# The modulation's products in four column quarters, and the state space part's transposes in one row

## The chip, the cores and the metric

The kernel runs on one core of one Trainium2 chip. The metric is the device time of one execution in microseconds. Three executions took 2125.67 to 2131.05 us, median 2130.01. A further execution was recorded by the hardware profiler; all durations below come from it.

TensorE does the matrix products and writes PSUM. VectorE (DVE), ScalarE (ACT) and GpSimd (POOL) work beside it, SyncE (SP) and GpSimd issue DMAs.

## The reference

Two layers of a diffusion trunk over 128 context tokens and 1024 latent tokens, 1024 features wide. What the change touches:

```python
def ada_mod(cvec, w, b):
    m = jax.nn.silu(cvec) @ w + b
    shift, scale, gate = jnp.split(m, 3, axis=-1)
...
    sh_p, sc_p, g_p = ada_mod(c_ctx[None], w_ada[l], b_ada[l])
    sh_s, sc_s, g_s = ada_mod(c, w_ada[l], b_ada[l])
    hp = rms_norm(xp, norm_w[l]) * (1.0 + sc_p) + sh_p
    hs = rms_norm(xs, norm_w[l]) * (1.0 + sc_s) + sh_s
```

So for each of the two layers two conditioning vectors of 1024 go through a matrix of 1024 x 3072. The first layer holds a bidirectional state space mixer with 16 heads of 64 in 128-token chunks:

```python
    y_diag = jnp.einsum('bhcls,bcshp->bclhp', scores, xdt)
    ...
    y_off = jnp.einsum('bclhn,bchpn->bclhp', cc, new_states[:, :-1]) * jnp.exp(acs).transpose(0, 2, 3, 1)[..., None]
    return (y_diag + y_off).reshape(b, L, h, p), new_states[:, -1]
```

and beside it a long convolution, an input projection and an output projection. The second layer is neighbourhood attention. All is fp32.

## The kernel before, in words

Activations are kept with features on the partitions, 1158 token columns in three pieces of 386. A projection multiplies weight tiles of 128 x 128 with these pieces. Each fp32 operand is split into a high and a low part of the type fp32r; three products (L158 to L160: high-high, high-low, low-high) replace one fp32 product.

The projections run as foreground. Everything else of the first layer is written as generators in a list `bg`; after each piece of a projection `tick` adds a rate to a credit and advances the first generator by as many steps as the credit holds. The finished order on each engine is then set by a scheduler that follows the dependences.

**The modulation.** Its matrix is cut into 24 blocks (12 for each layer) of 256 output columns, each in two halves of 512 input features, 128 partitions by 4 x 256. `ada_mm` keeps a column pair of the conditioning as the stationary operand and moves 256 weight columns. For the first eight blocks of layer 0 (`ada_block`, L295) the products are plain fp32, 8 per block, at the program's start: they give the shift and scale for the norm of the first layer's input. For the other 16 blocks `ada_gen` runs in the background of the projection of z. It splits each weight half into fp32r parts (L259 on ScalarE, L260 on VectorE) and does two products for each of 8 slices (L303, L304), with the conditioning's high and low part side by side as four stationary columns. `ada_row` (L309) copies the result, 2 or 4 rows of 256, to SBUF; for the gate of layer 1 it is also stored in DRAM (growd) for the last stage, `final`. `ada_cols` (L320) multiplies the rows with a small selection matrix, which sums high and low parts and turns rows into columns, and adds the bias.

At the start ScalarE squares the eight input tiles and VectorE adds them up (xacc, L1500); L340 sums them over the features, L355 spreads the reciprocal root over the partitions (`rstd_rep`), `make_h` makes the projection's operands, and L185 to L187 are the first projection.

**The state space part.** `ssd` runs in the background of the projection of x0 and the gate. For each chunk and each half of the heads it computes the part from the carried states with tokens on the partitions: two products (L1005), scaled and added on VectorE (yo, L1006 and L1008). This must be turned to features on the partitions. L1033 does so by a plain fp32 product with the identity, one for each pair of heads, into the PSUM bank yT, and the two products of that pair inside the chunk (L1037) accumulate on top, each into 64 partitions. Each group of four heads has its own masked decay on VectorE before that (ga, from the products L1014). L1038 reads the whole bank. Chunk 0, the context, has no carried state and no L1033.

Of the kernel before, what the change touches and what calls it, by code (L numbers as in the profile page):

```python
# [44 lines left out]
class Net:  # L45
# [148 lines left out]
    def open(self):  # L194
# [18 lines left out]
        self.sel4 = self.t(self.p_c, [4, 2], "sel4")  # L213
# [12 lines left out]
        self.growd = self.t(d, [4, 1024], "growd")  # L226
# [4 lines left out]
    def silu_c(self):  # L231
# [6 lines left out]
        s = self.cs = self.t(self.p_c, [128, 8, 2], "csl")  # L238
        nc.vector.scalar_tensor_tensor(out=s, in0=th, scalar=1.0, in1=c, op0=ALU.add, op1=ALU.mult)
        nc.vector.tensor_scalar(out=s, in0=s, scalar1=0.5, scalar2=None, op0=ALU.mult)  # L240
        self.ca = self.t(self.p_c, [128, 8, 4], "ca", F32R)
        nc.vector.tensor_copy(self.ca[:, :, 0:2], s)
        nc.vector.tensor_tensor(out=self.ca[:, :, 2:4], in0=s, in1=self.ca[:, :, 0:2].bitcast(F32), op=ALU.subtract)

    def ada_gen(self, blocks, pool):

        nc = self.nc
        todo = [(l, nb, half) for l, nb in blocks for half in range(2)]

        def load(i):  # L250
            r = self.t(pool, [128, 1024], "u8", bufs=self.nu8)
            l, nb, half = todo[i]
            self.dma(r, self.i["wada"][l, nb, half])
            return r
# [8 lines left out]
        raw = {0: load(0), 1: load(1)}  # L263
        yield
        hl = {0: split(0, raw.pop(0))}
        raw[2] = load(2)
        yield
        hl[1] = split(1, raw.pop(1))
        yield
        last = None  # L270
        for i, (l, nb, half) in enumerate(todo):
            if i + 3 < len(todo):
                raw[i + 3] = load(i + 3)
            if i + 2 < len(todo):
                hl[i + 2] = split(i + 2, raw.pop(i + 2))
            yield
            hi, lo = hl.pop(i)
            if half == 0:
                p = self.ps()
            self.ada_mm(p, half, hi, lo)  # L280
            if last:
                self.ada_cols(*last)
                last = None
            if half:
                last = l, nb, self.ada_row(l, nb, p, pool)
        self.ada_cols(*last)

    def ada_block(self, nb, raw, pool):

        nc = self.nc  # L290
        p = self.ps()
        for half, r in enumerate(raw):
            for k in range(4):
                kk = half * 4 + k
                nc.tensor.matmul(p[0:2, :256], self.cs[:, kk, :], r[:, k * 256:(k + 1) * 256], start=(kk == 0), stop=(kk == 7))  # L295
        return 0, nb, self.ada_row(0, nb, p, pool, 2)

    def ada_mm(self, p, half, hi, lo):
        nc = self.nc
        for k in range(4):  # L300
            kk = half * 4 + k
# [4 lines left out]
    def ada_row(self, l, nb, p, pool, n=4):  # L306

        row = self.t(pool, [4, 256], "w3")[0:n]
        self.nc.scalar.copy(row, p[0:n, :256])  # L309
# [4 lines left out]
    def ada_cols(self, l, nb, row):  # L314

        nc = self.nc
        n = row.shape[0]
        q = self.ps()
        for j in range(2):
            nc.tensor.matmul(q[:, 2 * j:2 * j + 2], row[:, j * 128:(j + 1) * 128], self.sel4[0:n], start=True, stop=True)  # L320
# [636 lines left out]
    def ssd(self, pool):  # L957
# [4 lines left out]
        for c in list(range(1, NCH)) + [0]:  # L962
# [35 lines left out]
            for g in range(2):  # L998
                yT = self.ps()
                if c:  # L1000
# [8 lines left out]
                    yield  # L1009
# [733 lines left out]
def constants():  # L1743
    import numpy as np

    f = np.float32
# [111 lines left out]
```

## Time and profile before

| | us |
|---|---|
| median of three executions | 2130.01 |
| profiled execution | 2134.96 |
| its span, first to last instruction | 2133.2 |
| TensorE busy | 2084.8 (98%) |
| VectorE busy | 1355.3 (64%) |
| ScalarE busy | 942.2 (44%) |
| GpSimd busy | 121.4 (6%) |

The program's start, with the first eight blocks, is about the first 90 us of the span. The 16 background blocks run from 334 to 441 us, the state space part from 883 to 1209 us, the attention from about 1455 us on. A plain fp32 matmul of the program leaves two records in the trace; an fp32r matmul leaves one. Matmuls are pipelined, so the time that one takes from TensorE's stream is the distance from its start to the next start, not its duration.

### The profile page before, as it was taken

What the parts mean: (1) busy time and instruction counts of PE and PEld (TensorE: products, weight loads), DVE (VectorE), ACT (ScalarE), POOL (GpSimd) and SP (SyncE); (2) the same over time, 40 slices, a digit from 0 to 9 for tenths busy, and PEclk for the clock granted to TensorE, in tenths of its full rate; (3) what the DMA queues carried; (4) which work ended last, traced back from release to release, by engine and by line L of the source; (5) the groups of instructions that cost most, each with busy time, mean ns of one, the idle gap of its engine ahead of it and who ended that gap; (6) DMA issues with size and microseconds to landing.
All of it is one profiled execution on the core that took longest, in us unless ns stands there. A gap on an engine that the chain in (4) does not pass through costs nothing.

```text
span 2133.2 us, 34117 instructions
## 1 busy us (share of the span) xinstructions
PE 2084.8 (98%) x13152; PEld 1870.8 (88%) x13152; DVE 1355.3 (64%) x2804; ACT 942.2 (44%) x2063; POOL 121.4 (6%) x241
## 2 busy tenths in 40 slices
PE   7999999999999999999999999999999999999998
PEld 3899998889999999888887899998888888888977
DVE  5797756544787778888788784563444444454364
ACT  3576553544233232554456621434444544543231
POOL 1110000010000000000000100200000000000000
PEclk8999999999999999999999999999999999999999
DMA  8133335765122113343334351243333223333452
GB/s 325 51 120 105 116 135 204 232 189 206 66 74 73 66 67 100 130 134 121 103 130 138 113 186 50 68 124 95 91 103 83 77 88 94 112 115 104 126 211 79
DMA packets 114945, 256.22 MB, mean 120 GB/s; under 512 B 27047, under 2 KB 63419, under 8 KB 112319
## 3 DMA queue, kind: packets, MB, share of 16 engines
q1 hardware_dynamic: 99472, 191.38, 28.8%
q0 software_dynamic: 15312, 62.67, 8.2%
q8 instruction: 104, 1.70, 0.3%
q14 instruction: 57, 0.47, 0.1%
HBM read 186.61 MB, written 67.38 MB: 119 GB/s over the span
## 4 chain that ended last, share of the span: by engine, by line
PE 36%; issue 21%; DMA 2%; DVE 2%; ACT 1%; POOL 1%; SPq 0%; POOLq 0%; DVEq 0%; ACTq 0%
PE pj L158 7%; PE pj L159 7%; PE pj L160 7%; PE bg L1037 1%; PE bg L1005 1%; PE pj L1377 1%; PE pj L1376 1%; PE pj L1378 1%; PE bg L1033 1%; PE bg L1014 1%; DMA yr<-yad 1%; PE bg L930 1%; PE bg L1339 1%; PE bg L1351 1%; DMA ycd<-X 1%
## 5 line engine op out<-in xcount | busy, mean ns | idle before, releaser
L158 PE MATMUL pj<-hh,whi 128*128 128x386 f32 x1728 | 603.0, 349 | 0.5 <-DVE acc L862 0.5
L159 PE MATMUL pj<-hl,whi 128*128 128x386 f32 x1728 | 590.2, 342 | 0.0
L160 PE MATMUL pj<-hh,wlo 128*128 128x386 f32 x1728 | 587.6, 340 | 0.0
L158 PEld LDWEIGHTS pj<-hh,whi 128*128 128x128 f32 x1728 | 326.4, 189 | 15.7 <-issue 12.9
L159 PEld LDWEIGHTS pj<-hl,whi 128*128 128x128 f32 x1728 | 326.7, 189 | 7.3 <-issue 6.2
L160 PEld LDWEIGHTS pj<-hh,wlo 128*128 128x128 f32 x1728 | 326.4, 189 | 3.5 <-issue 2.7
L131 DVE TENSOR_TENSOR wlo<-wraw,whi 128x1024 fp32r<-128x1024 f32 x108 | 131.8, 1222 | 165.5 <-ACT whi L130 158.9
L130 ACT CAST whi<-wraw 128x1024 fp32r<-128x1024 f32 x108 | 113.1, 1048 | 246.3 <-PE pj L159 213.3
L1255 DVE CUSTOM_DVE_ANT_0 sz<-bg,Tb 128x512 f32<-128x512 f32 x128 | 83.5, 688 | 127.8 <-PE bg L1322 127.2
L598 ACT COPY raw<-pj 128x386 f32<-128x386 f32 x105 | 50.5, 483 | 169.7 <-PE pj L160 82.6
L1257 ACT ACTIVATE sz<-sz,mx 128x512 f32<-128x512 f32 x128 | 91.5, 716 | 56.2 <-DVE mx L1255 56.0
L158 PE MATMUL pj<-yhi,whi 128*128 128x386 f32 x324 | 110.3, 340 | 1.4 <-DVE x L1094 1.4
L159 PE MATMUL pj<-ylo,whi 128*128 128x386 f32 x324 | 110.9, 342 | 0.0
L160 PE MATMUL pj<-yhi,wlo 128*128 128x386 f32 x324 | 110.4, 341 | 0.0
L1353 ACT COPY Pt<-bg 128x512 f32<-128x512 f32 (+1 forms) x144 | 71.9, 549 | 32.4 <-PE bg L1351 28.6
L1177 PE MATMUL pj<-whi,hh 128*128 128x256 f32 x288 | 83.3, 290 | 0.0
L1178 PE MATMUL pj<-wlo,hh 128*128 128x256 f32 x288 | 81.7, 284 | 0.0
L1179 PE MATMUL pj<-whi,hl 128*128 128x256 f32 x288 | 81.2, 282 | 0.0
L1351 PE MATMUL bg<-csq,sz 128*128 128x128 f32 x528 | 73.9, 280 | 0.0
L923 ACT ACTIVATE xw<-xt,wd 128x64 f32<-128x64 f32 x256 | 64.9, 336 | 14.1 <-PE bg L930 12.0
L1351 PEld LDWEIGHTS bg<-csq,sz 128*128 128x128 f32 x528 | 56.7, 140 | 13.0 <-issue 12.8
L1094 DVE SCALAR_TENSOR_TENSOR x<-pj,mod,x 128x128 f32<-128x128 f32 (+1 forms) x96 | 46.4, 512 | 29.6 <-PE pj L160 25.6
(428 smaller groups left out, 4254.6 us busy)
## 6 DMA issues: line engine op xcount, KB each, us to landing
wraw<-in_we SPq DMA_DIRECT2D x52, 512.0 KB, 4.2
u<-in_wada SPq DMA_DIRECT2D x34, 512.0 KB, 4.5
wraw<-in_wo SPq DMA_DIRECT2D x24, 512.0 KB, 3.6
Tb<-Cd SPq DMA_DIRECT2D x256, 48.0 KB, 2.0
Hd<-H POOLq DMA_DIRECT2D x8, 1280.0 KB, 5.6
H<-Hd SPq DMA_DIRECT2D x8, 1280.0 KB, 5.4
xt<-xtd SPq DMA_DIRECT2D x17, 512.0 KB, 4.6
wraw<-in_woe SPq DMA_DIRECT2D x16, 512.0 KB, 3.6
```

What stands on the lines that cost most here:

```text
L130: self.nc.scalar.copy(hi, r)
L131: self.nc.vector.tensor_tensor(out=lo, in0=r, in1=hi.bitcast(F32), op=ALU.subtract)
L158: nc.tensor.matmul(p[:, :NB], wh, xh[k][:, sl], start=(k == 0), stop=False)
L159: nc.tensor.matmul(p[:, :NB], wh, xl[k][:, sl], start=False, stop=False)
L160: nc.tensor.matmul(p[:, :NB], wl, xh[k][:, sl], start=False, stop=(k == nk - 1))
L1177: nc.tensor.matmul(p[:, :256], self.hh[k][:, ts], hi[:, q:q + 256], start=(k == 0), stop=False)
L1178: nc.tensor.matmul(p[:, :256], self.hh[k][:, ts], lo[:, q:q + 256], start=False, stop=False)
L1179: nc.tensor.matmul(p[:, :256], self.hl[k][:, ts], hi[:, q:q + 256], start=False, stop=(k == 7))
L1255: V.tensor_tensor_reduce(out=z[:, :n], in0=s, in1=tb, scale=-1.0, scalar=3.0e38, op0=ALU.add, op1=ALU.min, accum_out=m1)
L1257: nc.scalar.activation(z[:, :n], z[:, :n], AF.Exp, bias=m1, scale=-1.0, accum_out=sm)
L1351: nc.tensor.transpose(pt[:, b * 128:(b + 1) * 128], p[:, b * 128:(b + 1) * 128], self.ident)
L1353: nc.scalar.copy(t[:, :nb * 128], pt[:, :nb * 128])
```

## The change

**The modulation.** All 24 blocks now use plain fp32. The stationary operand is the conditioning pair padded with zeros to 32 columns (`cs`, made by `silu_wide`). Of the four slices of a half, slice k writes output partitions 32k to 32k + 31 of the same 256 columns, so the four work in four quarters of the array's columns. The second half adds to the first. The row copy is 128 x 256 instead of 2 or 4 x 256, and the selection matrix, now 128 x 2, sums the four quarters. The split into high and low parts is gone. `ada_gen` loads four halves ahead and two more per block into six buffers; it has one step for each half.

**The state space part.** The four transposes of a half of the heads stand in one row, after the step that follows yo's sum, with the transpose flag. The first of them has the start flag for the bank; the products L1037 (now L1023) accumulate on top.

```diff
-        self.sel4 = self.t(self.p_c, [4, 2], "sel4")
+        self.sel4 = self.t(self.p_c, [128, 2], "sel4")
...
-        self.growd = self.t(d, [4, 1024], "growd")
+        self.growd = self.t(d, [128, 1024], "growd")
...
+    def silu_wide(self, pool):
+
+        V = self.nc.vector
+        self.cs = self.t(pool, [128, 8, 32], "cw", bufs=1)
+        V.memset(self.cs, 0.0)
+        V.tensor_copy(self.cs[:, :, 0:2], self.sc)
 
     def ada_gen(self, blocks, pool):
 
-        nc = self.nc
+        self.silu_wide(pool)
         todo = [(l, nb, half) for l, nb in blocks for half in range(2)]
...
-        def split(i, r):
-            t = self.t(pool, [128, 2048], "F", F32R, 3)
-            hi, lo = t[:, 0:1024], t[:, 1024:2048]
-            nc.scalar.copy(hi, r)
-            nc.vector.tensor_tensor(out=lo, in0=r, in1=hi.bitcast(F32), op=ALU.subtract)
-            return hi, lo
...
+        def load(i):
+            if i < len(todo):
+                raw[i] = self.t(pool, [128, 1024], "wa", bufs=6)
+                l, nb, half = todo[i]
+                self.dma(raw[i], self.i["wada"][l, nb, half])
+
+        for i in range(4):
+            load(i)
         yield
         last = None
-        for i, (l, nb, half) in enumerate(todo):
...
+        for i, (l, nb) in enumerate(blocks):
+            load(2 * i + 4)
+            load(2 * i + 5)
+            p = self.ps()
+            self.ada_mm(p, 0, raw.pop(2 * i))
             yield
...
+            self.ada_mm(p, 1, raw.pop(2 * i + 1))
             if last:
                 self.ada_cols(*last)
...
+            last = l, nb, self.ada_row(l, nb, p, pool)
+            yield
         self.ada_cols(*last)
...
-    def ada_mm(self, p, half, hi, lo):
-        nc = self.nc
...
+    def ada_mm(self, p, half, w):
+
         for k in range(4):
-            kk = half * 4 + k
-            ks = slice(k * 256, (k + 1) * 256)
-            nc.tensor.matmul(p[0:4, :256], self.ca[:, kk, :], hi[:, ks], start=(kk == 0), stop=False)
-            nc.tensor.matmul(p[0:4, :256], self.ca[:, kk, :], lo[:, ks], start=False, stop=(kk == 7))
...
+            self.nc.tensor.matmul(p[32 * k:32 * k + 32, :256], self.cs[:, half * 4 + k, :], w[:, k * 256:(k + 1) * 256],
+                                  start=(half == 0), stop=(half == 1))
...
-        row = self.t(pool, [4, 256], "w3")[0:n]
-        self.nc.scalar.copy(row, p[0:n, :256])
+        row = self.t(pool, [128, 256], "w3")
+        self.nc.scalar.copy(row, p[:, :256])
...
                     V.tensor_tensor(out=yo[:, 0], in0=yo[:, 0], in1=yo[:, 1], op=ALU.add)
                     yield
+
+                    for mm in range(4):
+                        nc.tensor.matmul(yT[:, mm * 128:(mm + 1) * 128], yo[:, 0, mm * 128:(mm + 1) * 128], self.ident,
+                                         start=(mm == 0), stop=False, is_transpose=True, skip_group_check=True)
...
-                        if c:
-                            nc.tensor.matmul(ys, yo[:, 0, mm * 128:(mm + 1) * 128], self.ident, start=True, stop=False)
...
-                            nc.tensor.matmul(ys[64 * s:64 * s + 64], x[:, h * 64:h * 64 + 64], a[:, hh], start=(c == 0), stop=True)
+                            nc.tensor.matmul(ys[64 * s:64 * s + 64], x[:, h * 64:h * 64 + 64], a[:, hh], start=(c == 0), stop=True, skip_group_check=True)
```

`ada_block` calls the same `ada_mm` for the first eight blocks. In `final` the selection matrix and the stored rows have 128 partitions instead of 4.

How the finished order moves is shown at three places. First TensorE in the background modulation, before: the rows L303 and L304 are the products of a block's two halves, bg_3277 their PSUM tile, L320 the selection matmuls of the block before. Four such pairs stand on each side of it; one is shown.

```order
L303 MATMUL bg_3277<-F_3192,ca_105 4x256
L304 MATMUL bg_3277<-F_3192,ca_105 4x256
L320 MATMUL bg_3286<-sel_7_82,w_500_3244 128x2 x2
L303 MATMUL bg_3277<-F_3233,ca_105 4x256
L304 MATMUL bg_3277<-F_3233,ca_105 4x256
```

And after: L288 are the quarter products (x4: four alike), L304 the selection, L611 and L612 the foreground (the projection of the step sizes).

```order
L612 MATMUL pj_3267<-hl_144_647,wdts_3263 64x386
L288 MATMUL bg_3254<-wa_3164,cw_3151 32x256 x4
L304 MATMUL bg_3289<-sel_7_82,w_503_3248 128x2 x2
L288 MATMUL bg_3299<-wa_3204,cw_3151 32x256 x4
L611 MATMUL pj_3304<-hh_112_378,wdts_3263 64x386
L612 MATMUL pj_3304<-hl_113_379,wdts_3263 64x386
```

The two halves of a block stand on both sides of a foreground piece, each in a group of four, and the selection matmuls of the earlier block stand between two such groups.

Second, TensorE in the state space part, before: yo is the operand to be transposed, ga and xt those of the products inside the chunk, bg_7993 the bank yT.

```order
L160 MATMUL pj_8267<-hh_112_378,wlo_8082 128x386
L1033 MATMUL bg_7993<-csq_72,yo_7994 128x128
L1014 MATMUL bg_8093<-Mv_7885,L_7884 128x512
L1014 MATMUL bg_8094<-Mv_7885,L_7884 128x512
L1005 MATMUL bg_8147<-S_1135_7926,ct_7932 128x512
L1005 MATMUL bg_8150<-sb_7936,ct_7932 128x512
L1037 MATMUL bg_7993<-ga_8037,xt_7928 64x128 x2
L1033 MATMUL bg_7993<-csq_72,yo_7994 128x128
L1037 MATMUL bg_7993<-ga_8037,xt_7928 64x128 x2
L1033 MATMUL bg_7993<-csq_72,yo_7994 128x128
L1014 MATMUL bg_8181<-Mv_7885,L_7884 128x512
```

And after: the transposes are L996, the products inside the chunk L1023 (elsewhere in the stream), L1002 what was L1014.

```order
L158 MATMUL pj_8731<-hh_143_646,whi_8529 128x386
L159 MATMUL pj_8731<-hl_144_647,whi_8529 128x386
L160 MATMUL pj_8731<-hh_143_646,wlo_8530 128x386
L996 MATMUL bg_8722<-csq_72,yo_8723 128x128 x4
L1002 MATMUL bg_8762<-Mv_7664,L_7663 128x512
L1002 MATMUL bg_8763<-Mv_7664,L_7663 128x512
L158 MATMUL pj_8780<-hh_112_378,whi_8529 128x386
```

The four transposes of a half of the heads now stand together ahead of the decay's products, and none stands among the products inside the chunk.

Third, ScalarE at the program's start, before: L1498 squares the input tiles hl, L309 copies a block's row w.

```order
L237 ACT_TABLE_LOAD
L237 ACTIVATE cth_100<-cT_98 128x16
L1498 ACTIVATE xacc_132<-hl_27_124 128x1158
L1498 ACTIVATE hh_55_198<-hl_28_125 128x1158
L309 COPY w_54_195<-bg_186 2x256
L400 ACT_TABLE_LOAD
```

And after, with L1485 for the squares and L294 for the row copy:

```order
L237 ACT_TABLE_LOAD
L237 ACTIVATE cth_100<-cT_98 128x16
L294 COPY w_54_195<-bg_186 128x256
L1485 ACTIVATE xacc_132<-hl_26_121 128x1158
L1485 ACTIVATE hh_55_198<-hl_27_122 128x1158
L294 COPY w_58_214<-bg_205 128x256
```

The first row copy has moved ahead of the first two squares.

## Rows read from the trace of the kernel before

**Rows 1.** The page, part 1: busy time, share of the span, instructions

```profile
PE 2084.8 (98%) x13152; PEld 1870.8 (88%) x13152; DVE 1355.3 (64%) x2804; ACT 942.2 (44%) x2063; POOL 121.4 (6%) x241
```

**Rows 2.** Busy time of each engine in two stretches, from the windows view

```profile
420.00:440.00 20.00, 20.00 (x133) 17.73 (x132) 8.66 (x13) 7.56 (x11) 4.17 (x7) 1.00 0.66 170
920.00:940.00 20.00, 20.00 (x117) 16.66 (x115) 18.58 (x47) 6.91 (x13) 0.54 (x1) 1.00 0.48 151
```

**Rows 3.** Timeline of TensorE (start us, duration us) in the background modulation

```profile
338.93 0.28 PE L303 MATMUL bg<-F,ca 128*4 128x256 f32 x1
...
339.95 0.60 PE L320 MATMUL bg<-sel,w 4*128 4x2 f32 x4
340.49 0.28 PE L303 MATMUL bg<-F,ca 128*4 128x256 f32 x1
...
341.40 0.34 PE L627 MATMUL pj<-hh,wdts 128*64 128x386 f32 x1
```

**Rows 4.** Timeline of TensorE in the attention, around L1339

```profile
1507.55 0.34 PE L159 MATMUL pj<-hl,whi 128*128 128x386 f32 x1
1507.73 0.34 PE L160 MATMUL pj<-hh,wlo 128*128 128x386 f32 x1
1507.99 0.88 PE L1339 MATMUL bg<-Pt,vw 128*64 128x128 f32 x12
1508.70 0.39 PE L1339 MATMUL bg<-Pt,cv 128*64 128x128 f32 x4
1509.02 0.44 PE L158 MATMUL pj<-hh,whi 128*128 128x386 f32 x1
1509.29 0.34 PE L159 MATMUL pj<-hl,whi 128*128 128x386 f32 x1
```

**Rows 5.** Timeline of TensorE at the start of the program

```profile
39.41 3.97 PE L340 MATMUL bg<-csq,xacc 128*128 128x1 f32 x18 [6.04 <-DVE xacc L1500]
...
44.25 6.48 PE L295 MATMUL bg<-F,csl 128*2 128x256 f32 x16
50.66 2.20 PE L355 MATMUL bg<-diag,csq 128*128 128x384 f32 x6
...
53.33 3.61 PE L295 MATMUL bg<-F,csl 128*2 128x256 f32 x16
56.87 0.81 PE L185 MATMUL pj<-hh,whi 128*128 128x386 f32 x3
```

**Rows 6.** Timeline of VectorE at the start of the program

```profile
37.91 1.36 DVE L1500 TENSOR_TENSOR xacc<-xacc,hh 128x1158 f32<-128x1158 f32 x1
...
47.59 1.03 DVE L352 TENSOR_TENSOR diag<-csq,rs 128x384 f32<-128x384 f32 x2 [1.72 <-POOL rs L346]
```

**Rows 7.** Timeline of TensorE in the state space part

```profile
898.77 0.38 PE L1033 MATMUL bg<-csq,yo 128*128 128x128 f32 x2
898.91 0.71 PE L1014 MATMUL bg<-Mv,L 128*128 128x512 f32 x2
...
1118.54 0.44 PE L1037 MATMUL bg<-ga,xt 128*64 128x128 f32 x4 [0.36 <-DVE ga L1027]
1118.91 0.49 PE L1033 MATMUL bg<-csq,yo 128*128 128x128 f32 x2
1119.33 0.44 PE L1037 MATMUL bg<-ga,xt 128*64 128x128 f32 x4
...
1192.39 0.66 PE L1037 MATMUL bg<-ga,xt 128*64 128x128 f32 x8
1192.97 1.18 PE L1014 MATMUL bg<-Mv,L 128*128 128x512 f32 x4
```

**Rows 8.** Timeline of TensorE in the attention: a run of eight transposes

```profile
1500.08 1.09 PE L1351 MATMUL bg<-csq,sz 128*128 128x128 f32 x8
1500.93 0.42 PE L158 MATMUL pj<-hh,whi 128*128 128x386 f32 x1
```

**Rows 9.** Waits ahead of L1037 (releaser: us in all, times)

```profile
  DVE ga L1027: 4.9, 13
```

More of the change, by code (lines that the diff above doesn't have):

```diff
@@ L245, in ada_gen @@
     def ada_gen(self, blocks, pool):
-        nc = self.nc
+        self.silu_wide(pool)
         todo = [(l, nb, half) for l, nb in blocks for half in range(2)]
+        raw = {}
         def load(i):
[L251 to L254, printed above, removed]
-        def split(i, r):
-            t = self.t(pool, [128, 2048], "F", F32R, 3)
-            hi, lo = t[:, 0:1024], t[:, 1024:2048]
-            nc.scalar.copy(hi, r)
-            nc.vector.tensor_tensor(out=lo, in0=r, in1=hi.bitcast(F32), op=ALU.subtract)
-            return hi, lo
@@ L291, in ada_block @@
         p = self.ps()
         for half, r in enumerate(raw):
-            for k in range(4):
-                kk = half * 4 + k
-                nc.tensor.matmul(p[0:2, :256], self.cs[:, kk, :], r[:, k * 256:(k + 1) * 256], start=(kk == 0), stop=(kk == 7))
-        return 0, nb, self.ada_row(0, nb, p, pool, 2)
-    def ada_mm(self, p, half, hi, lo):
-        nc = self.nc
-        for k in range(4):
-            kk = half * 4 + k
-            ks = slice(k * 256, (k + 1) * 256)
-            nc.tensor.matmul(p[0:4, :256], self.ca[:, kk, :], hi[:, ks], start=(kk == 0), stop=False)
-            nc.tensor.matmul(p[0:4, :256], self.ca[:, kk, :], lo[:, ks], start=False, stop=(kk == 7))
@@ L306, in ada_row @@
-    def ada_row(self, l, nb, p, pool, n=4):
-        row = self.t(pool, [4, 256], "w3")[0:n]
-        self.nc.scalar.copy(row, p[0:n, :256])
+            self.ada_mm(p, half, r)
+        return 0, nb, self.ada_row(0, nb, p, pool)
+    def ada_mm(self, p, half, w):
+        for k in range(4):
+            self.nc.tensor.matmul(p[32 * k:32 * k + 32, :256], self.cs[:, half * 4 + k, :], w[:, k * 256:(k + 1) * 256],
+                                  start=(half == 0), stop=(half == 1))
+    def ada_row(self, l, nb, p, pool):
+        row = self.t(pool, [128, 256], "w3")
+        self.nc.scalar.copy(row, p[:, :256])
@@ L316, in ada_cols @@
         nc = self.nc
-        n = row.shape[0]
         q = self.ps()
         for j in range(2):
-            nc.tensor.matmul(q[:, 2 * j:2 * j + 2], row[:, j * 128:(j + 1) * 128], self.sel4[0:n], start=True, stop=True)
+            nc.tensor.matmul(q[:, 2 * j:2 * j + 2], row[:, j * 128:(j + 1) * 128], self.sel4, start=True, stop=True)
         m = self.mod[l][0].rearrange("p a k s -> p (a k) s")[:, 2 * nb:2 * nb + 2, :]
@@ L1368, in final @@
         gr = self.t(pool, [128, 2, 1024], "gater", bufs=1)
-        sel4b = self.t(pool, [4, 2, 128], "sel4b", bufs=1)
+        sel4b = self.t(pool, [128, 2, 128], "sel4b", bufs=1)
         self.dma(sel4b, self.i["sel4b"])
-        rows = self.t(pool, [4, 1024], "x1t")
+        rows = self.t(pool, [128, 1024], "x1t")
         self.dma(rows, self.growd)
@@ L1750, in constants @@
     o["c_sq"] = np.stack([r == c, r <= c, r >= c, r > c, r < c, r >= 0 * c], 1).astype(f)
-    s4 = np.zeros((4, 2), f)
-    s4[[0, 2], 0] = 1
-    s4[[1, 3], 1] = 1
-    o["sel4"] = s4
-    o["sel4b"] = np.repeat(s4[:, :, None], 128, 2)
+    s4 = np.zeros((4, 32, 2), f)
+    s4[:, 0, 0] = s4[:, 1, 1] = 1
+    o["sel4"] = s4.reshape(128, 2)
+    o["sel4b"] = np.ascontiguousarray(np.repeat(o["sel4"][:, :, None], 128, 2))
     o["sel64"] = np.tile(np.eye(32, dtype=f), (2, 1))
```

23 lines of the change are left out of this document (2 added, 21 removed).

## Prediction

> **What bounds the kernel now.** I read the page's engine totals first. TensorE is busy for 2084.8 of 2133.2 us, 98% [rows 1], so I price whatever leaves or joins its stream in full, unless another engine is close behind. The table by stages comes second. From 420 to 440 us, where the background modulation runs, TensorE is busy for all of 20 us and VectorE for 8.66. From 920 to 940 us, in the state space part, TensorE is again full, but VectorE has 18.58 us [rows 2]. So the first stage can keep all it saves, the second perhaps not. Third is TensorE's timeline, read by the distance from one start to the next. A record's own duration includes the pipeline and overlaps its neighbours.
>
> **Part 1, the background modulation (16 blocks).** Today a block is 16 one-pass matmuls of 256 columns plus the two selection matmuls (four records). From one L303 start to the projection behind the block it takes 341.40 - 338.93 = 2.47 us, of which the selection's records take 340.49 - 339.95 = 0.54 [rows 3]. Sixteen blocks are 39.5 us.
>
> Afterwards a half is four plain fp32 matmuls in four column quarters, each of two records. The trace has no quarters. It has halves: L1339 writes output partitions 0 to 63 and 64 to 127 in turn. Its 16 records start at 1507.99 and the next work starts at 1509.02, so 1.03 us for 16 records of 128 columns, 0.064 each [rows 4]. What a plain fp32 record costs alone stands at the start of the program, where today's first blocks are plain fp32 too: 16 records of 256 columns from 53.33 to 56.87, 0.22 each, so 0.11 for 128 columns [rows 5]. At 0.064, two halves run at once. I assume that four quarters do too: four records together take 0.22, and the two records of each quarter follow one another, so 0.44 us a half.
>
> Column groups have a price at their borders. L1339 starts 0.26 after the L160 before it, where L160 itself started 0.18 after its forerunner. Its 16 records should take 8 x 0.11 = 0.88 and take 1.03, and the matmul behind keeps its successor waiting 0.27 instead of 0.18 [rows 4]. That is 0.08 + 0.15 + 0.09 = 0.32 us a visit. Today's narrow matmuls show none of it: eight of them take 0.91 us up to the next projection's start (340.49 to 341.40), 0.114 each, near half of a plain record's 0.22 [rows 3, 5].
> The Trainium skill, page "TensorEngine Tiling (Array Packing)", section Key Properties, says that changing the tiling mode (not just the tile) drains the TensorE, and gives no price. With no border cost a block would be 2 x 0.44 + 0.44 = 1.32 us and the stage would save 18.4 us. With the rows' 0.32 it saves 8.2. The trace agrees that there is a price and gives its size; I go by the rows.
>
> The order shows that the two halves of a block mostly stand apart, with the selection matmuls between one block's second half and the next block's first, so each half is one visit. Selection now has 128 rows in place of 4, the same four records, and stays a full-array shape: four records at the transposes' 0.11 (part 3) are 0.44. A block is then 2 x (0.44 + 0.32) + 0.44 = 1.96 us, against 2.47: 16 x 0.51 = **8.2 us saved**. Bounds: 18.4 saved without borders, and a loss of 34 if the quarters take turns (below). The value taken is nearest to the only row with column groups.
>
> The 32 casts on ScalarE and 32 subtractions on VectorE that made high and low parts go away. I count them as nothing: both engines are busy for under half of that stage [rows 2], so TensorE's stream covers them. The weight loads stay on SyncE's queue, four to six ahead instead of three. A load that waits for a buffer there holds back projection weights behind it, but the buffer comes free with a product two half-blocks back, so I expect no wait; a wait would delay a projection weight that is used for 13 us (72 matmuls of 0.18). The stores of the gate rows are 128 rows instead of 4; they stand on GpSimd's queue and are read only in the last stage.
>
> **Part 2, the first eight blocks.** A block of 16 records takes 3.6 us at speed (53.33) [rows 5]. In quarters it is 4 x 0.22 + 0.32 = 1.2, so 2.4 saved where TensorE bounds. The first four end before L340, which starts at 39.41 and had waited for the sum of squares, whose last addition VectorE began at 37.91 [rows 5, 6]. VectorE gets there through its sine layer and the inputs' arrival, so I give these four only 0.5 us. ScalarE's order now has the first row copy ahead of the first two squares (the order rows show it), and the copy must wait for the first block's products, 1.2 us of work or about twice that at the start's slower pace. That may push the squares by some 2 us, and VectorE's queue absorbs it or not: 2 us more or less.
> The fifth block (44.25) took 6.48 us and holds L355, whose first operand VectorE began at 47.59 [rows 5, 6]. L355 can start about 2 us earlier than 50.66, but may run slower there, as the fifth block itself did (6.48 for the same work as 3.61); I take 1.5. The sixth (53.33) ends at 56.87, where the first projection starts at once [rows 5]; its operand is being made beside the block, so I count 1 of the 2.4. The last two stand among projections: 2 x 2.4 = 4.8, less a microsecond as VectorE's making of the operands follows close behind. Together **7 us**, from 1 to 10.
>
> **Part 3, the transposes.** Per group of four heads the trace shows L1037 0.37 (1118.54 to 1118.91), L1033 0.42 (to 1119.33), L1037 0.37 again, and the group's first L1033, which stands after a full-array matmul, 0.14 (898.77 to 898.91) [rows 7]. Sum 1.30, times 32 groups (8 chunks of 4) is 41.6 us. L1033 is slow twice: plain fp32 needs two records, and it makes L1037 enter and leave column halves once more in each group.
> The chunk that has no L1033 (c = 0) shows what will be left: eight L1037 records in 0.58 us (1192.39 to 1192.97) [rows 7]. To this 0.08 for entering from a projection [rows 4]. In place of L1033 there are 64 transposes in rows of four. The attention's transposes have the same operands and shape: eight in 0.85 us, 0.106 each [rows 8], and one record each. So 32 x 0.66 + 64 x 0.106 + 16 x 0.05 at a row's start = 28.7 us, and 41.6 - 28.7 = 12.9 us come free on TensorE.
> How much stays depends on VectorE. At 93% in the fullest stretch [rows 2] it would need more than TensorE in places once 5% of TensorE's work is gone. Between 0 (all of it turns into waits for VectorE) and 12.9, I take **10**: most of this stage's stretches are less full than the one shown. The transposes need VectorE's sum of both directions all four at once, where today only the first does. In the order the row of four stands 12 to 64 matmuls behind the last product that the sum needs, 2 us at the least at 0.18 each; I expect it to wait in a few places only. What would wait behind it is TensorE's whole stream.
>
> **Sum.** 8.2 + 7 + 10 = 25 us. The profiled execution took 2134.96 us, its span 2133.2; 25 less is 2110. The runs' median is 2130.01, 5 below that execution, so I forecast **2105 us** for the median.
>
> **The rivals.**
> A. *Quarters overlap only in pairs.* For it: the trace shows nothing beyond two groups at once. Against: in L1339 both groups reach the full rate, with no sign of a shared limit. A half is then 0.88 + 0.32 = 1.20, a block 2.84: 16 x 0.37 = 6 us lost; the first blocks save 4; with 10 from the transposes the time is 2122.
> The Trainium skill, page "TensorE: Matmul & The Clock Gate", section "Measured speedup vs the span model", has 2.38 times for three column tiles of 32; by that a half would cost about a quarter more than I assume, and by this estimate the sum would be some 3.5 us less. The trace has no such tiles, so no row bears on it.
> B. *VectorE takes the transposes' gain.* For it: the 93%, and L1037 has waited for its operand 13 times already. Against: those 13 waits are 4.9 us in all [rows 9]. With 2 of the 10 left: 2113.
> C. *Slower: the quarters take turns.* The place is the fp32 products' issue: if a quarter must finish both its records before the next starts, a half is 8 x 0.22 + 0.32 = 2.08, a block 4.6, 16 x 2.13 = 34 us lost, the first blocks gain nothing, and 10 from the transposes leave 2154. It decides from the point where a quarter's record costs over 0.13 us on average (16 x (2 x (8 x 0.13 + 0.32) + 0.44 - 2.47) is 11 us lost), against the 0.055 assumed. Against it: L1339's two groups do run at once.
> D. *The transposes are not one pass* (the flag changes only arithmetic): then they cost two records each as today, and only the order is gained, about 6 instead of 10: 2109, inside the forecast.
>
> **How the numbers follow.** Forecast with D 0.72 (own range 2097 to 2113), A 0.10, B 0.11, C 0.05, and 0.02 for something unseen. The range 2094 to 2123 takes in A and B; most of C and the far end, where borders cost little, stay out. A change below 0.3% (6.4 us) can't be told from none in this kernel. Slower than that is C and a rest: 0.06. Within it is the bad ends of A and B: 0.07. Faster: 0.87.
>
> **What would show it.** The records of the quarter products should start four together and come every 0.22 us; pairs show A, single file C. A block with its selection should take about 2 us. The transposes should be 64 records, 0.106 apart, and L1037's group 0.58 us. If B holds, waits of the state space matmuls for VectorE grow by several microseconds. L340's successor should start within 2 us of 39.41; if it moves far earlier, I have the first stage's limit wrong.

## The result and the profile after

The changed kernel took 2101.23 us (median of 4 runs, 2097.59 to 2103.47) against 2130.53 (4 runs, 2125.67 to 2136.81): ratio 0.9859, 95% interval 0.983 to 0.9889. Forecast 2105, range 2094 to 2123. The profiled executions stand further apart than the medians, 2133.2 to 2099.9 us of span, because that of before lay 4.4 us above its median.

Where the 33.3 us went can be counted. Every kernel of this study issues the same 6156 products L158 to L160 in the same order, so the start of the n-th of them is a milestone that all share. This table, worked out from the timelines, gives in us what each stretch took more or less than in the kernel before. The labels are those of the experiments below; e12 is the changed kernel once more.

| stretch, up to the n-th product (its start before) | after | e12 | e1 | e2 | e3 | e4 | e5 | e6 | e10 | e8 | e11 | e7 | e13 |
|---|---|---|---|---|---|---|---|---|---|---|---|---|---|
| start, to the 1st (93.4) | -2.9 | -5.6 | 0.0 | -5.8 | -5.1 | -5.7 | -3.5 | -3.2 | -0.3 | -5.7 | -7.7 | -2.5 | -8.3 |
| filter part, to the 601st (293.4) | 0.0 | 0.4 | -0.2 | 0.3 | 0.4 | 0.2 | 0.0 | 0.4 | -0.1 | 0.7 | -0.1 | 1.6 | 1.2 |
| background modulation, to the 1401st (510.3) | -13.5 | -13.5 | -1.2 | -13.5 | 5.0 | 20.0 | -13.5 | -11.3 | -13.3 | -12.7 | -12.0 | -13.6 | -14.5 |
| convolutions, to the 2701st (872.2) | -0.2 | -0.7 | -1.4 | -1.1 | -1.5 | -1.3 | -1.5 | -1.3 | -1.3 | -1.7 | -0.7 | -0.2 | -0.1 |
| state space, to the 3951st (1245.9) | -16.0 | -15.2 | -16.5 | -1.9 | -17.9 | -17.1 | -7.5 | -7.9 | -17.4 | -17.4 | -17.5 | -17.7 | -15.8 |
| the rest, to the last (2016.0) | 1.4 | -0.7 | 0.8 | 3.6 | -1.0 | -2.7 | -2.5 | 1.6 | -0.2 | 1.3 | -0.3 | 2.4 | -0.8 |

The 117 us behind the last of these products hold the 2 us that are missing to 33.3. Stretches that nothing was changed in move by up to 3.6 us from one execution to the next; a smaller difference is read below only where rows of the trace show where it comes from.

Lines moved by the change: L303/L304 and L295 are now L288, L320 is L304, L340 L324, L355 L339, L1033 L996, L1037 L1023, L1014 L1002. The first line of the page, against [rows 1], then the two kinds of stretch of [rows 2] (the second is the state space part's, 15 us earlier as it has moved; columns as there):

```profile
PE 2041.4 (97%) x13088; PEld 1839.9 (88%) x13088; DVE 1316.7 (63%) x2774; ACT 908.3 (43%) x2031; POOL 120.4 (6%) x241
```

```profile
420.00:440.00 20.00, 20.00 (x110) 18.85 (x110) 4.63 (x10) 4.74 (x10) 2.00 (x3) 1.00 0.19 64
905.00:925.00 20.00, 20.00 (x120) 16.77 (x121) 18.16 (x43) 7.68 (x13) 0.55 (x1) 1.00 0.41 126
```

TensorE is still the engine that is full, and VectorE stands at 91% in that stretch, not above it.

TensorE's timeline in the background modulation (start, duration), against [rows 3]:

```profile
382.06 0.33 PE L160 MATMUL pj<-hh,wlo 128*128 128x386 f32 x1
382.33 0.64 PE L288 MATMUL bg<-wa,cw 128*32 128x256 f32 x8
382.90 0.61 PE L304 MATMUL bg<-sel,w 128*128 128x2 f32 x4
383.43 0.64 PE L288 MATMUL bg<-wa,cw 128*32 128x256 f32 x8
384.00 0.44 PE L158 MATMUL pj<-hh,whi 128*128 128x386 f32 x1
384.28 0.33 PE L159 MATMUL pj<-hl,whi 128*128 128x386 f32 x1
```

A half is eight records in 0.57 us (382.33 to 382.90), the selection 0.53. From L160 to the second product behind the block pass 384.28 - 382.06 = 2.22 us where two products alone need 0.35: the block costs **1.87 us**. By the same measure a block before cost 2.49 (most of its 16). All runs of these lines between 320 and 450 us, entering and leaving included, sum to 40.2 us before and 29.0 after.

The start of the program, against [rows 5]:

```profile
39.53 3.97 PE L324 MATMUL bg<-csq,xacc 128*128 128x1 f32 x18 [8.57 <-DVE xacc L1487]
...
48.33 4.18 PE L339 MATMUL bg<-diag,csq 128*128 128x384 f32 x6 [2.11 <-DVE diag L336]
...
55.82 0.88 PE L185 MATMUL pj<-hh,whi 128*128 128x386 f32 x3 [1.72 <-ACT hh L361]
...
60.04 0.53 PE L186 MATMUL pj<-hl,whi 128*128 128x386 f32 x1
60.37 0.52 PE L187 MATMUL pj<-hh,wlo 128*128 128x386 f32 x1
```

L324 starts where L340 did. What follows begins 2.3 us earlier and is slower: L339 takes 4.18 instead of 2.20, and the first projection's products come every 0.32 us instead of 0.18.

The state space part, a row of transposes and a group of four heads, against [rows 7]; under them the waits ahead of L996 and of L1023 (one line and two of the lists), against [rows 9]:

```profile
879.66 0.34 PE L158 MATMUL pj<-hh,whi 128*128 128x386 f32 x1
879.83 0.60 PE L996 MATMUL bg<-csq,yo 128*128 128x128 f32 x4
880.18 0.71 PE L1002 MATMUL bg<-Mv,L 128*128 128x512 f32 x2
...
885.15 0.33 PE L159 MATMUL pj<-hl,whi 128*128 128x386 f32 x1
885.41 0.66 PE L1023 MATMUL bg<-ga,xt 128*64 128x128 f32 x8
886.00 0.45 PE L160 MATMUL pj<-hh,wlo 128*128 128x386 f32 x1
886.29 0.34 PE L158 MATMUL pj<-hh,whi 128*128 128x386 f32 x1
```

```profile
  DVE yo L992: 1.4, 4
```

```profile
  DVE ga L1015: 3.4, 12
...
  DVE ga L1010: 2.0, 6
```

Four transposes take 0.35 us, 0.09 apart, one record each. A group costs 886.29 - 885.15 - 0.35 = 0.79 us between projections. Before, 18 of the 32 groups stood in one piece, as here (eight L1037 and two L1033), and the other 14 had their first L1033 apart:

```profile
901.69 0.34 PE L158 MATMUL pj<-hh,whi 128*128 128x386 f32 x1
901.96 0.44 PE L1037 MATMUL bg<-ga,xt 128*64 128x128 f32 x4
...
903.37 0.42 PE L159 MATMUL pj<-hl,whi 128*128 128x386 f32 x1
903.63 0.34 PE L160 MATMUL pj<-hh,wlo 128*128 128x386 f32 x1
```

By the same measure this group costs 1.59 us; the seven of the 18 that stand, like it, between two of the products L158 to L160 cost 1.58 or 1.59. TensorE waits for VectorE a little more than before: 3.4 + 2.0 + 1.4 = 6.8 us, against 4.9 and, ahead of the same products, 0.5 for the line that is now L1010:

```profile
  DVE ga L1022: 0.5, 2
```

### The profile page after: what moved, and what is told of

It reads as the page before. It is cut to its first block, busy times and chain, and to the rows that moved or that the text cites. A ratio compares the mean times of both kernels' runs of the same rounds, so it can differ in the third digit from the quotient of the medians.

```text
span 2099.9 us, 33885 instructions
## 1 busy us (share of the span) xinstructions
PE 2041.4 (97%) x13088; PEld 1839.9 (88%) x13088; DVE 1316.7 (63%) x2774; ACT 908.3 (43%) x2031; POOL 120.4 (6%) x241
## 4 chain that ended last, share of the span: by engine, by line
PE 36%; issue 20%; DVE 3%; DMA 2%; ACT 1%; POOL 1%; SPq 0%; POOLq 0%; DVEq 0%; ACTq 0%
PE pj L158 7%; PE pj L159 7%; PE pj L160 7%; PE pj L1363 1%; PE pj L1364 1%; PE pj L1362 1%; PE bg L989 1%; PE bg L1023 1%; PE bg L1002 1%; PE bg L1325 1%; PE bg L1337 1%; PE bg L914 1%; PE pj L186 1%; PE bg L1308 1%; PE pj L187 0%
## 5 line engine op out<-in xcount | busy, mean ns | idle before, releaser
L158 PE MATMUL pj<-hh,whi 128*128 128x386 f32 x1728 | 604.2, 350 | 0.8 <-DVE acc L846 0.8
L160 PE MATMUL pj<-hh,wlo 128*128 128x386 f32 x1728 | 589.5, 342 | 0.0
L158 PEld LDWEIGHTS pj<-hh,whi 128*128 128x128 f32 x1728 | 326.2, 189 | 21.4 <-issue 18.0
L160 PEld LDWEIGHTS pj<-hh,wlo 128*128 128x128 f32 x1728 | 326.1, 189 | 5.3 <-issue 4.5
L158 PE MATMUL pj<-yhi,whi 128*128 128x386 f32 x324 | 110.1, 340 | 0.0
L160 PE MATMUL pj<-yhi,wlo 128*128 128x386 f32 x324 | 109.7, 339 | 0.0
L1339 ACT COPY Pt<-bg 128x512 f32<-128x512 f32 (+1 forms) x144 | 71.9, 549 | 32.0 <-PE bg L1337 28.2
L1337 PEld LDWEIGHTS bg<-csq,sz 128*128 128x128 f32 x528 | 56.6, 140 | 13.0 <-issue 12.7
```

The lines of the kernel that those rows point to most:

```text
L158: nc.tensor.matmul(p[:, :NB], wh, xh[k][:, sl], start=(k == 0), stop=False)
L160: nc.tensor.matmul(p[:, :NB], wl, xh[k][:, sl], start=False, stop=(k == nk - 1))
L1337: nc.tensor.transpose(pt[:, b * 128:(b + 1) * 128], p[:, b * 128:(b + 1) * 128], self.ident)
L1339: nc.scalar.copy(t[:, :nb * 128], pt[:, :nb * 128])
```

## The experiments

Ratios are to the kernel before, with their 95% interval. The changed kernel's own median was 2101.23 in one set of runs and 2097.3 in another, so kernels are compared by their ratios or within a set.

**Each part by itself (e1, e2).** e1 is the kernel before with the transposes' edit alone, e2 the changed kernel with the transposes taken back:

```
 e1, on before:                                     e2, on after:
+ for mm in range(4): nc.tensor.matmul(yT[..],      - the row of four
+     .., is_transpose=True)   # ahead of the heads + if c: nc.tensor.matmul(ys, yo[..], ident,
- if c: nc.tensor.matmul(ys, yo[..], ident, ..)     +     start=True, stop=False)  # between the halves
```

> The kernel before with part 3 alone: the four transposes in one row, one pass, ahead of the heads' products; the modulation as before. Theory 1 (the trace of after: from the start of the state space stage to its end the two kernels move apart by 16 us): about 16 us faster than before, 2114. The prediction's own term (10 us kept of 12.9 freed): 2120. Rival B (VectorE takes the gain back): about 2 us, 2128. Under theory 1 a group's four heads cost 0.79 us between projections instead of 1.35 to 1.58.

> The changed kernel with the transposes as they were before: parts 1 and 2 alone. Theory 1 (the traces: 3 us at the start, 11 in the background modulation, 2 to 3 in the order of the work behind it): 14 to 17 us faster than before, 2113 to 2116. The prediction's terms: 8.2 and 7, so 2115. Rival (the modulation's gain was shown only because the state space part ran better behind it): under 10 us, over 2120. If the parts add up, this and the kernel with the rows alone make about 30 us together.

e1: 2115.05 us, 0.9932 (0.9916 to 0.9949). e2: 2114.84, 0.9929 (0.9915 to 0.9944). Each part gives half, and the two make 30.3 us together where the change gave 29.3: they add up. In the table the transposes' gain stands in the state space stretch alone (-16.5 in e1, -1.9 in e2), the quarters' in the first and third. Theory 1 holds; the prediction's 10 us for the transposes was too small, and rival B (2 us) falls.
The 1.9 us of e2 in the state space stretch are no gain of the quarters. The execution of before lost them itself, at one place: e2 keeps step with it up to 1099 us and has gained 2.5 us on it by 1139. Between 1130 and 1140 us TensorE was busy for only 8.32 of 10 us in before, at a granted clock of 0.83. So the transposes' gain in the stretch is better counted from e2. TensorE's busy time in the whole stretch, in e2 and then after:

```profile
852.10:1223.80 371.70, 367.44 (x2043) 312.49 (x2043) 314.41 (x624) 199.46 (x471) 16.04 (x34) 1.00 0.40 132
855.50:1213.10 357.60, 350.35 (x1979) 301.54 (x1979) 314.49 (x625) 198.34 (x471) 16.06 (x34) 1.00 0.42 137
```

TensorE has 17.1 us less to do and 3.0 us more idle time, which leaves 14.1; counted from e2, all kernels with the flagged row come to between 13 and 16 us, and e1's runs to 15.

**How many quarters run at once (e3, e4).** e3 writes two halves of 64 columns in place of four quarters, e4 all 128 columns in file (background blocks only):

```
 e3: - p[32 * k:32 * k + 32, :256], cs[.., 32 wide]
     + p[64 * (k % 2):64 * (k % 2) + 64, :256], cs[.., 64 wide]
 e4: + p[:, :256], cs[.., 128 wide]
```

> The changed kernel with the modulation's products in two halves of the columns (64 wide, two products one after the other in each) instead of four quarters. Theory 1 (four quarters run at once, so that four records cost what one costs): a half of a block takes 0.57 + 0.44 = 1.0 us to the next record in place of 0.57; 32 x 0.44 = 14 us in the background, 2 to 3 at the start: 2117 to 2118. Rival A (quarters overlap only in pairs): no difference, 2101, and 0.57 for a half.

> The changed kernel with the 16 background blocks' products over all 128 columns (operand padded to 128 columns, no column groups, eight records in file for a half); the first eight blocks stay in quarters. Theory 1: 8 x 0.22 = 1.76 us a half, without the price of entering and leaving column groups (some 0.2 a visit): a block 2 x 1.76 + 0.5 = 4.0 instead of 1.87, 16 x 2.15 = 34 us slower than the changed kernel, 2135. Rival (most of a visit's 0.57 us is the border, and records of this shape run faster in file): a half under 1.2 us and 2115 or less.

e3: 2113.01 us, 0.9923 (0.9909 to 0.9938). e4: 2129.39, 0.9996 (0.9986 to 1.0005). TensorE's timeline of a block in e3, then in e4 (where L288 and L304 are L289 and L309):

```profile
382.28 1.08 PE L288 MATMUL bg<-wa,cw 128*64 128x256 f32 x8
383.29 0.61 PE L304 MATMUL bg<-sel,w 128*128 128x2 f32 x4
383.83 1.08 PE L288 MATMUL bg<-wa,cw 128*64 128x256 f32 x8
384.84 0.44 PE L158 MATMUL pj<-hh,whi 128*128 128x386 f32 x1
```

```profile
392.18 1.89 PE L289 MATMUL bg<-wa,cw 128*128 128x256 f32 x8
393.91 0.50 PE L309 MATMUL bg<-sel,w 128*128 128x2 f32 x4
394.27 1.97 PE L289 MATMUL bg<-wa,cw 128*128 128x256 f32 x8
395.89 0.53 PE L158 MATMUL pj<-hh,whi 128*128 128x386 f32 x1
```

The same eight records take 0.57 us in quarters, 1.01 in pairs and 1.73 in file. Pairs cost 0.44 more, two records of 0.22, as four at once demand: rival A falls. A whole block, from projection to projection, costs 1.87, 2.76 and 3.90 us. Sixteen times 2.03 is 32.5; the stretch differs by 33.5 (20.0 against -13.5). The medians differ by less than that, 28 us, with an interval of 6 us either way on the changed kernel's side. The profiled executions differ by 25: the start and the last stretch of e4 came out 2.8 and 4.1 us better than in the profile of after, which executions of one kernel also do. e4 has no casts either, and its stretch is 20 us longer than before: it is not the casts' end that makes the quarters' gain.
The border can be estimated from these. In file, 16 records next to each other take 3.27 us and the rest of a block 0.63. With a half and a quarter of the 3.27, the pairs' block has 2.76 - 1.63 - 0.63 = 0.50 left for its two visits and the quarters' 1.87 - 0.82 - 0.63 = 0.42: 0.21 to 0.25 a visit by this estimate, where the prediction had 0.32.

**The flag and the place (e5, e6).** e5 keeps the row and drops the transpose flag; e6 keeps the flag and puts each transpose back between the heads' products:

```
 e5: - start=(mm == 0), stop=False, is_transpose=True
     + start=(mm == 0), stop=False
 e6: - the row of four
     + if c: nc.tensor.matmul(ys, yo[..], ident, start=(mm == 0), stop=False, is_transpose=True)
```

> The changed kernel with the row of four transposes as plain fp32 products (no transpose flag): the order alone. Theory 1 (the flag makes a transpose one pass, 0.089 us apart in the trace of after; plain ones take two records): a row costs 0.35 us more, 16 rows 5.7 us, 2107. Rival D (the flag changes only the arithmetic): no difference, 2101. Rival B (VectorE sets the pace there, so TensorE's saving is not seen): 2102 with a row of twice the length.

> The changed kernel with the flagged transposes back in their old place, each ahead of its two heads' products, between the column halves: the flag alone, with the borders as before. Theory 1 (each transpose between halves costs a border of some 0.2 us beside its record; 32 groups lose one or two visits): about half of part 3's 16 us goes, 2108 to 2110. If the flag is all: 2101. If the order is all: 2115, as with the quarters alone.

e5: 2107.35 us, 0.9895 (0.9878 to 0.9911). e6: 2106.13, 0.9893 (0.9876 to 0.991). The row in e5, and a group in e6 (there L1017 is the transpose and L1022 the heads' products):

```profile
1069.91 1.06 PE L996 MATMUL bg<-csq,yo 128*128 128x128 f32 x8
1070.72 0.48 PE L1002 MATMUL bg<-Mv,L 128*128 128x512 f32 x1
```

```profile
993.74 0.34 PE L160 MATMUL pj<-hh,wlo 128*128 128x386 f32 x1
993.91 0.27 PE L1017 MATMUL bg<-csq,yo 128*128 128x128 f32 x1
994.12 0.44 PE L1022 MATMUL bg<-ga,xt 128*64 128x128 f32 x4
...
995.11 0.44 PE L158 MATMUL pj<-hh,whi 128*128 128x386 f32 x1
995.39 0.34 PE L159 MATMUL pj<-hl,whi 128*128 128x386 f32 x1
```

Without the flag a row is eight records in 0.81 us instead of four in 0.35, so rival D falls: the flag halves the records. In the old place this group (two transposes and eight products of heads) costs 1.30 us (995.39 - 993.74 - 0.35), against 0.79 and half a row of 0.35 in the changed kernel, 0.97. By the rows the flag is worth 16 x 0.46 = 7.4 us and the place some 9 (32 groups of 1.22 to 1.31 us there, against 0.97). In the stretch e5 and e6 lack 8.5 and 8.1 of the 16.0 us (-7.5 and -7.9), so flag and place are worth about 8 us each there. By the ratios each lacks 0.0034 to 0.0036, 7 us (5 to 6 beside e10, which has the row and ran in the same set), with intervals that touch or overlap: the split rests on the stretch and the rows.

**The start (e10, e7, e11).** e10 has the first eight blocks as before:

```
- p[32 * k:32 * k + 32, :256], cs, ..          # first eight blocks only
+ p[0:2, :256], sc, ..                         # two columns, 16 plain records a block
```

> The changed kernel with the first eight blocks as before (two columns wide, 16 plain records a block); the background blocks stay in quarters. Theory 1 (the start gave 3 us in the trace of after and 4.6 to 5.5 in those of the kernels that share it): 2104 to 2107. The prediction's term (7 us): 2108. Rival (the lower clock at the start takes back all that the quarters give there): 2101, with a granted clock of 0.8 or more between 40 and 70 us.

2101.22 us, 0.9863 (0.9847 to 0.9879): in the runs no difference from the changed kernel. In the table the start gives nothing there (-0.3) and 2.9 to 5.8 in the others with quarters and nothing added. The intervals are 5 us wide and more; what the first blocks give is seen in the trace and not shown by the runs. The granted clock between 40 and 70 us suggests why it is less than 7. The rows are before, e10, after and e12, in this order:

```profile
40.00:70.00 30.00, 30.00 (x129) 17.93 (x130) 20.38 (x36) 13.67 (x22) 10.91 (x25) 0.83 0.40 135
```

```profile
40.00:70.00 30.00, 29.62 (x133) 18.41 (x134) 21.58 (x38) 13.96 (x23) 13.01 (x25) 0.86 0.40 139
```

```profile
40.00:70.00 30.00, 26.17 (x142) 19.49 (x142) 17.50 (x33) 10.87 (x19) 10.69 (x23) 0.67 0.37 135
```

```profile
40.00:70.00 30.00, 26.18 (x158) 19.98 (x159) 19.85 (x35) 13.47 (x22) 11.07 (x25) 0.77 0.37 136
```

With 16 plain records TensorE is all but full from 40 us on, and the clock is back at 2.4 GHz (1.00) by about 50 us, as in before and e1. With quarters and nothing added TensorE has 4 us of idle time in the same stretch, and the clock is back at 52 to 54 us. In three of these executions (after, e5, e6) it then falls once more, from about 56 to 63 us, through the first projection; these are the ones whose start gave 2.9 to 3.5 us, where e2, e4, e8 and e12 gave 5.6 to 5.8. So e7 and e11 fill that idle time with products that nobody reads:

```
+ def warm(n, r):                      # e7: both operands constants; e11: r a late weight tile
+     for j in range(n): nc.tensor.matmul(q, self.ident, r[:, 512:1024], start=True, stop=True)
+ warm(7 or 8)       # ahead of the sum of squares
+ warm(2), warm(1)   # ahead of L339 and of the first projection
```

> The changed kernel with eleven more products that nobody reads (512 columns, identity by constants) in the waits of the first stage: eight ahead of the sum of squares, two ahead of the scale's spreading, one ahead of the first projection. Theory 1 (after, TensorE runs at half its clock from 35 to 51 us and again to 63 us, granted 0.67 between 40 and 70 us, and this takes back most of what the quarters save there): the granted clock stays near 1, the sum of squares takes about 2 us instead of 3.97, the first projection starts 3 to 4 us earlier and runs at 0.18 us a product; 5 us faster than the changed kernel, 2096. Rival (VectorE and ScalarE set that stage's end whatever TensorE's clock): 2100 to 2101.

e7: 2102.66 us, 0.9868 (0.9851 to 0.9885). It tested nothing: with constant operands the products were placed by their readiness, at 4.12 to 14 us and around 18, ahead of everything, and the sum of squares' products start at 41.63 with them, 2 us late.

> The changed kernel with ten unread products (512 columns) in the waits of the first stage; their operands are weight tiles that arrive late, so that they stand in the order where the waits are (in the earlier try they were put ahead of everything). Theory 1 (a lower clock from 31 to 63 us takes back what the quarters give at the start): the clock stays near 1 to 40 us and behind, L324 takes about 2 us instead of 3.97, the first projection starts at 52 instead of 55.8, 4 to 5 us faster than the changed kernel, 2096. Rival (the chain through VectorE and ScalarE sets that stage's end; the plain start, which ran at full clock from 50 us, gained nothing either): the first projection's end within 1 us of 2.5 us less, 2100 to 2101.

e11: 2095.08 us, 0.9843 (0.983 to 0.9857), beside 2097.3, 0.9853 (0.9839 to 0.9866) for the changed kernel in the same set (e12). Its start:

```profile
30.98 6.28 PE L1473 MATMUL pj<-hh,csq 128*128 128x512 f32 x14
39.63 3.88 PE L324 MATMUL bg<-csq,xacc 128*128 128x1 f32 x18 [2.37 <-DVE xacc L1492]
...
49.73 2.22 PE L339 MATMUL bg<-diag,csq 128*128 128x384 f32 x6
...
55.17 0.77 PE L185 MATMUL pj<-hh,whi 128*128 128x386 f32 x3 [0.82 <-POOL hl L366]
```

L339 is back at 2.22 us and the first projection starts 1 us earlier than in e12 (56.26) and half a microsecond before the changed kernel's first profile (55.82). L324 did not get faster: its granted clock is 0.50 from 40 to 50 us in spite of the six microseconds of full work ahead of it. The stretch gained 2.1 us on e12, of 4 to 5 that theory 1 expected, and in e13, which has the same products, 2.7; that the rest of the chain is VectorE's and ScalarE's is argued, not shown. The medians don't separate the two.

**One visit instead of two (e8, e12, e13).** e8 puts a block's two halves behind each other:

```
- self.ada_mm(p, 0, raw.pop(2 * i))
  yield
+ self.ada_mm(p, 0, raw.pop(2 * i))
  self.ada_mm(p, 1, raw.pop(2 * i + 1))
```

> The changed kernel with both halves of a background block right behind each other, so that a block enters and leaves the column groups once instead of twice. Theory 1 (a visit has a border; the pairs and the full width put it at some 0.3 us): a block 1.87 - 0.13 to 0.3, so 1.6 to 1.74 us between projections, 2 to 5 us faster than the changed kernel in the background stage: 2097 to 2099. Rival (only the change to and from the selection costs, and it stays): no difference in the stage, 2101.

> The changed kernel itself, once more, beside the two others: 2101, and a second look at its start (the trace of after had 3 us less than before there, those of kernels that share the start 4.6 to 5.5). If the start varies from run to run with the clock, it shows another value than 3.

> The changed kernel with both: halves of a block behind each other, and the ten unread products at the start. If the two gains are there and add up: 6 to 9 us faster than the changed kernel, 2092 to 2095. If only one is: 2096 to 2099.

e8: 2096.12 us, 0.9848 (0.9835 to 0.9862). e12: 2097.3. e13 (both): 2096.05, 0.9851 (0.9838 to 0.9865). None of the three is shown to beat the changed kernel. In e8's rows a visit less is worth what was expected:

```profile
387.57 1.07 PE L288 MATMUL bg<-wa,cw 128*32 128x256 f32 x16
388.57 0.61 PE L304 MATMUL bg<-sel,w 128*128 128x2 f32 x4
389.04 0.42 PE L158 MATMUL pj<-hh,whi 128*128 128x386 f32 x1
```

A block costs 1.64 us from projection to projection, 0.23 less, and all of them sum to 26.4 instead of 29.0. Yet the stretch gave 12.7, not more than 13.5. The granted clock (last but two) of 345 to 355 us, in e12 and then in e8, shows where it went:

```profile
345.00:355.00 10.00, 10.00 (x78) 8.46 (x78) 5.88 (x12) 1.79 (x4) 0.28 (x1) 1.00 1.02 357
```

```profile
345.00:355.00 10.00, 10.00 (x47) 9.92 (x48) 5.09 (x9) 0.81 (x2) 0.54 (x1) 0.66 1.01 339
```

In e8 the clock fell to 1.2 GHz for some microseconds although TensorE was never idle: what it did there is the block, its selection and then L619, 18 records of 32 columns. At 0.66 for 10 us about 3.4 us are lost, more than the 2.6 that the blocks saved.
The order of the halves is not what makes it fall. Of the fourteen traces five have a fall at this place, during those 18 records or within 1.3 us behind the last: besides e8 also e13 (0.66 from 345 to 350 us), e11 (0.83 from 345 to 355), e6 (0.83 from 350 to 360), and the kernel before, whose row is this:

```profile
350.00:360.00 10.00, 10.00 (x60) 9.20 (x58) 6.03 (x9) 3.11 (x5) 0.00 (x0) 0.83 0.63 205
```

At 0.83 for 10 us 1.7 are lost. e6 and e11 have the changed kernel's modulation, and their stretches lack 2.2 and 1.5 of its 13.5 us. Compared with like, the visit's saving is there in the stretch: e13 and e11 both have one such fall, and e13, with the halves behind each other, is 2.5 us shorter (-14.5 against -12.0). Why the clock falls there in some executions and not in others is open.

## Why the prediction was right, and where it was not

**The sum.** 25 us were forecast, 29.3 came. The forecast's own range (2097 to 2113) held the median. Its terms were further off than its sum: two too small, one too large. Parts 1 and 2 were to give 15.2 us together, and e2's runs give 15.3; that is luck, as the first was too small by about as much as the second was too large.

**Part 1, 8.2 us forecast; 13.5 in the stretch.** The mechanism was right in each step: four at once, 0.22 for four records, a price at the borders, the casts' end hidden. The price was taken from the attention's row, 0.32 a visit, and is 0.21 to 0.25; the selection takes 0.53 and not 0.44. A block of 1.96 was forecast and 1.87 measured; before, it was 2.49 where the prediction had 2.47. That makes 16 x 0.62 = 9.9, and 11.2 over all visits, since some blocks stood split in more visits before. Some 2 us more came in the same stretch outside the blocks. Most of them are the kernel before's own: its clock fell at 354 us, and e1, with the same modulation and no fall there, took 1.2 us less. In e3 that rest is of the other sign (its clock fell behind the blocks, 0.89 from 475 to 490 us), so it is no property of the quarters.
The Trainium skill, page "TensorE: Matmul & The Clock Gate", section "Measured speedup vs the span model", gives 2.38 times for three column tiles; an estimate from this is 0.79 a tile. Here four gave 1.73 / 0.57 = 3.0 times with a border inside, 0.76 a tile, so the trace comes close to that estimate. Part of what is missing to four times is the border: 16 records right behind each other take 1.00 us in e8 against 3.27 in file, 3.3 times.

**Part 2, 7 us forecast; 2.9 to 5.8 in the traces, not shown in the runs.** The first four blocks gave nothing of their 0.5 us: L324 starts within 0.12 us of L340, for the reason that was given, since it still waits for the sum of squares. ScalarE's earlier copy pushed nothing by more than that (VectorE's last addition begins at 38.02 us, in the kernel before at 37.91). What failed is the step that priced the fifth and sixth at 1.5 and 1 us: up to the first projection 3 us were forecast with the 0.5, and 0.6 (e12) to 1.1 us (after) came. L339 begins 2.3 us earlier and takes 2 us longer, and the first projection then waits 1.7 us for ScalarE's operand. The warning that L355 "may run slower there" was right, and the price took too little account of it. From there to the first of the products L158 (93.4 us before), where the last two blocks stand, 3.8 us were forecast; 5.0 came in e12, where the first projection ran at 2.4 GHz, and 1.9 in the first profile, where it ran at 1.2.

**Part 3, 10 us kept of 12.9 forecast; 15.2 to 17.9 measured.** The step that failed is the sum of 41.6 us. It added the records of L1033 and L1037 and left out what the same visits cost at their ends, while the sum after had part of that in it. From projection to projection a group cost 1.58 us before where it stood in one piece between products L158 to L160, and 1.35 and 0.14 where its first L1033 stood apart: 1.54 in the mean, not 1.30. After, it costs 0.79 and half a row of 0.35, so 0.97, not 0.90. Thirty-two times 0.57 is 18 us free; by the busy time it was 17.1. Counted from e2, 13 to 16 of these were kept, about as large a share as the forecast's 10 of 12.9. TensorE was idle for 3.0 us more, part of it the waits for VectorE (6.8 us against 5.4): rival B's place was right and its size a fraction.

**The rivals.** A: its price for the stretch was right (6 us lost forecast, 5.0 in e3), its condition is not met. C: the quarters do not take turns. In file by its code (e4) a block costs 3.90 us where C had 4.6, since records in file come every 0.20 to 0.22 us and pay no border. D fell with e5.

## What to carry to other kernels

Price a visit to a part of the array from projection to projection, on both sides of the comparison: the records' own distances left out some 0.2 us a visit, and here that was 5 of the 18 us that the transposes set free. The narrow plain products here, each filling a quarter of the columns, ran four at once, three times as fast as in file even in runs of eight. A stage that is freed of TensorE's work while it waits for other engines may give part of the gain back through the granted clock, as the start did here; look at that column before counting on the gain, and in the kernel before too: a fall in its own profile looks like a gain of the change.

## What was not expected of the hardware

The same program got another clock in another execution: in the changed kernel's first profile the first projection's products came every 0.32 us up to 62.9 us, in e12's every 0.18 from 58.4 on, and the start took 2.7 us less. And in five of fourteen traces the clock fell to 1.2 GHz around 350 us with TensorE busy all the time, during 18 narrow records or close behind them; the other nine have the same records and no fall.
A stretch of full work did not keep the clock either: in e11, 14 records of 512 columns (6.28 us) end 2.4 us ahead of L324, and the clock is at 1.2 GHz from 40 to 50 us, through L324's 18 records of one column. The Trainium skill, page "TensorE: Matmul & The Clock Gate", section "Part 1: The HAM clock gate", says that the clock follows the array's recent activity and that the point of its rise varies from run to run. The rows agree with the second, and the points of its fall vary too. The falls around 350 us, where TensorE was never idle, are not explained by these rows.
